# The scan of an RWKV-7 mixer: two recurrences side by side, another form of the recurrence, and other queues, banks and estimates

## The chip, the cores and the metric

The kernel runs on one core of one Trainium2 chip. The metric is the device time of one execution in microseconds (us), lower is better; the times shown are the median of several runs. TensorE (PE in the profile, PEld for its weight loads) multiplies matrices into PSUM, VectorE (DVE), ScalarE (ACT) and GpSimd (POOL) do the elementwise work, SyncE (SP) issues the DMA transfers.

## The reference

A four-layer encoder over 16 meta tokens and 512 tokens (T = 528 rows of 1024 features). The mixers of its layers are latent attention (MLA), RWKV-7, a gated linear recurrence and again MLA; behind each mixer comes a gated feed-forward network. The change is in the RWKV-7 mixer, whose heart is a recurrence over the tokens, for 16 heads of 64 features and in both directions:

```python
def _wkv7_scan(r, w, a, b, k, v, reverse):
    def step(S, inp):
        r_t, w_t, a_t, b_t, k_t, v_t = inp
        sa = jnp.einsum('bhvk,bhk->bhv', S, a_t)
        S = S * w_t[:, :, None, :] + sa[..., None] * b_t[:, :, None, :] + v_t[..., None] * k_t[:, :, None, :]
        return S, jnp.einsum('bhvk,bhk->bhv', S, r_t)
    ...
# in the mixer, for d in range(2):
        ys.append(_wkv7_scan(rf, decay, -kk, kk * a, kd, vf, reverse=(d == 1)))
        bonuses.append(jnp.sum(rf * kd * r_k_h, axis=-1, keepdims=True) * vf)
    y = ys[0] + ys[1]      # then normalised per head, plus the bonuses, gated, projected
```

## The kernel before

The kernel computes the recurrence in chunks of 64 tokens ("windows": NW = 8 full ones and a ninth of 16 tokens, N9 = 9). Two heads share the 128 partitions (a "pair", hp = 0 to 7; E[0] and E[1] are its halves), so a pair and a direction d make one **recurrence**, i = 2 hp + d, 16 in all. Nearly all its products are 64x64 by 64 columns in float32, one per head.

For each recurrence there are these streams of work, written as Python generators:

- `pair` loads r, k and v of two heads; `values` turns v to have tokens on partitions (vt).
- `stage_a` (line 1505) makes decays and the scaled r, a (xr) and b, k (bk), then in six PSUM banks the products of all tokens of a window with each other (am: for b and for k, against a and r), masked by VectorE.
- `a_tokens` turns a (at), `bk_tokens` turns b and k (tb), each with `turned`: a product with the identity per window and head, then copies on ScalarE. `ak_v` makes r1, am times v.
- `inverses` (line 1600) sends the 16x16 diagonal blocks of am through DRAM to 66 partitions (sc, bu), inverts them there in 30 small GpSimd operations (dt, dtmp) and sends them back (sd, dc).
- `stage_b` (line 1638) builds from dc the inverse X of the 64x64 triangle (dd, nn, xt) by four products in the one bank "rb", and xa = X times a.
- `chain` (line 1679) walks the nine windows. One step: u = X r1 + xa S (TensorE, then VectorE's copy), S' = decay times (S + k v + b u) (TensorE, then VectorE, with the product sp of S and the decay on GpSimd), and the output y from v, S and u in the bank "yp". `chain` of i waits for that of i - 1.
- `bonus` and `post` finish a pair.

**Order.** `Streams` (line 140 on) puts the streams into one program order per engine while the program is built: of the next operations of all streams it takes the one that by its estimates (`Op`: a cost by engine and size, LATENCY between engines, `after` for a DMA's landing) can start first, and among equals the one of highest priority (AHEAD[kind] - i). `take` and `give` hand out PSUM banks by kind; `wait` keeps a stream back until other streams are fully put in order. In line 1537 `stage_a` of i waits so for `chain` of i - DEEP; tiles of depth DEEP (xr, am, tb, pc) back it. On the chip each engine then runs its own list in order and waits where an operand is late. Where the estimates leave TensorE idle, `fill` puts in matmuls nobody reads, so far into a bank "idle" of their own. The eight PSUM banks are ps 3, ch 2, rb 1, yp 1, idle 1. The MLA mixers use the same `Streams` with their own streams. All DMA transfers are issued by SyncE, in the same program order.

Of the kernel before, what the change touches and what calls it, by code (L numbers as in the profile page):

```python
# [50 lines left out]
DEEP = 3  # L51
# [54 lines left out]
class Op:  # L106
    __slots__ = ("eng", "fn", "args", "kw", "outs", "ins", "cost", "work", "after", "mode")

    def __init__(self, eng, fn, name, args, kw):
# [6 lines left out]
        if eng == "pe":  # L116
# [27 lines left out]
class Streams:  # L144
# [19 lines left out]
    def wait(self, *names):  # L164
        return ("wait", names)
# [111 lines left out]
    def fill(self, start):  # L277
# [48 lines left out]
class Kern:  # L326
# [1034 lines left out]
    def rwkv_scan(self, es, hid, rkv, yall):  # L1361
# [14 lines left out]
        for kind, n in (("ps", 3), ("ch", 2), ("rb", 1), ("yp", 1)):  # L1376
# [4 lines left out]
        idle, dense = pp.tile([128, 512], F32, name="idle"), hid["w", 0]  # L1381
# [18 lines left out]
        xts = [cp.tile([128, N9, 64], F32, name=f"xt{j}") for j in range(2)]  # L1400
# [61 lines left out]
        def turned(src, out):  # L1462

            yield from per_window(lambda w, e: src(w)[E[e]], lambda w, e: self.ident[E[e], E[e]], lambda ps, ws: ac.copy(out[:, ws], ps))


        def pair(hp, P):
            if hp >= 2:
                yield wait(f"bonus{hp - 2}")
            for n, name in ((2, "v"), (0, "r")):  # L1470
                P[name] = tl([128, T], "in_" + name, 2)
                yield dq.dma_start(P[name], rkv[n, hp])
# [3 lines left out]
            yield dq.dma_start(P["k"], rkv[1, hp])  # L1476
# [28 lines left out]
        def stage_a(i, hp, d, P, U):  # L1505
            if i:
                yield wait(f"front{i - 1}")
            if d == 0:
                raw = tl([128, 512], "w2")
                yield dq.dma_start(raw, a["rw_2"][hp, :, 0:512])  # L1510
# [41 lines left out]
            yield spawn(f"at{i}", a_tokens(i, xr, U), prio("at", i))  # L1552
# [27 lines left out]
            yield spawn(f"r1{i}", ak_v(i, hp, P, U), prio("r1", i))  # L1580
            if d:
                yield po.tensor_tensor(out=P["kds"], in0=P["kds"], in1=kd, op=ALU.add)

        def a_tokens(i, xr, U):
            if i >= 2:
                yield wait(f"b{i - 2}")
            U["at"] = tl([128, N9, 64], "at", 2)
            yield from turned(lambda w: xr[:, 0, w * 64:w * 64 + 64], U["at"])
# [6 lines left out]
        def ak_v(i, hp, P, U):  # L1595
            yield wait(f"values{hp}", *([f"c{i - 3}"] if i >= 3 else []))
            r1 = U["r1"] = tl([128, N9, 64], "r1", 3)
# [336 lines left out]
```

## Time and profile before

| | us |
|---|---|
| median of 3 runs (3481.07 to 3485.17) | 3481.4 |
| the profiled execution | 3473.31 |
| its span, first to last instruction | 3471.5 |
| TensorE busy in the span | 3216.4 (93%) |
| VectorE busy | 2701.7 (78%) |
| ScalarE busy | 1673.0 (48%) |
| GpSimd busy | 936.7 (27%) |

The profile has one row per instruction: engine, line of the kernel, the tiles written and read (out<-in), start and length. The streams record their operations through one helper, so all of them have line L218, and tiles tell them apart. A float32 product shows as two TensorE instructions. TensorE's instructions overlap in its pipeline, so the distance between two starts is what one costs, not its length.

### The profile page before, as it was taken

The numbers are of one execution on the slowest core, as the hardware profiler recorded it, in microseconds if no ns is written. First come the engines' busy times: TensorE is split into PE (matmuls) and PEld (weight loads), VectorE is DVE, ScalarE is ACT, GpSimd is POOL, SyncE is SP. The second block draws the span as 40 slices with busy tenths as digits, with TensorE's granted clock in tenths as the row PEclk, the third lists the DMA queues.
The fourth block names the chain that finished last, engine by engine and source line by source line (L and its number), as shares of the span: only waits on it lengthen the run. The fifth ranks groups of instructions, "written<-read, shape, count | busy, mean of one in ns | idle before, by whom it ended". The sixth has DMA issues, their size and how long they took to land.

```text
span 3471.5 us, 77910 instructions
## 1 busy us (share of the span) xinstructions
PE 3216.4 (93%) x32057; PEld 3099.1 (89%) x32057; DVE 2701.7 (78%) x5006; ACT 1673.0 (48%) x3139; POOL 936.7 (27%) x1406
## 2 busy tenths in 40 slices
PE   7999999997988988879999988989999899989998
PEld 7899899996977878869999988989999799989998
DVE  6877789979336767657898788789886777788987
ACT  6665454433333333224544468654444666554443
POOL 0000143422016555433443200044331000034431
PEclk9999999998989999989999999999999999999999
DMA  2001223322322112113323222222322011112322
GB/s 84 34 33 40 84 71 104 99 87 88 136 69 50 35 40 45 25 42 102 98 95 107 80 73 74 80 73 88 106 86 83 21 38 35 65 64 83 101 93 72
DMA packets 157717, 250.07 MB, mean 72 GB/s; under 512 B 78736, under 2 KB 88112, under 8 KB 157232
## 3 DMA queue, kind: packets, MB, share of 16 engines
q1 hardware_dynamic: 157360, 245.08, 22.4%
q8 instruction: 252, 4.13, 0.5%
q14 instruction: 105, 0.86, 0.1%
HBM read 227.93 MB, written 17.10 MB: 71 GB/s over the span
## 4 chain that ended last, share of the span: by engine, by line
PE 47%; DVE 10%; ACT 6%; issue 2%; POOL 2%; DMA 2%; SPq 0%; DVEq 0%; ACTq 0%; POOLq 0%
PE bank L422 11%; PE bank L421 11%; PE bank L420 11%; PE pj L218 4%; PE ps L218 2%; PE s L218 1%; PE ch L218 1%; PE rb L218 1%; PE yp L218 1%; PE mm L420 1%; PE mm L421 1%; PE mm L422 1%; POOL dt L218 1%; ACT wv L218 1%; ACT th L1227 1%
## 5 line engine op out<-in xcount | busy, mean ns | idle before, releaser
L421 PE MATMUL bank<-xlo,whi 128*128 128x264 f32 x2272 | 655.7, 290 | 18.7 <-DVE xlo L562 10.9
L422 PE MATMUL bank<-xhi,wlo 128*128 128x264 f32 x2272 | 651.2, 289 | 12.4 <-DVE wlo L409 12.3
L420 PE MATMUL bank<-xhi,whi 128*128 128x264 f32 x2272 | 646.6, 289 | 15.4 <-ACT whi L408 13.8
L421 PEld LDWEIGHTS bank<-xlo,whi 128*128 128x128 f32 x2272 | 437.0, 192 | 26.1 <-DVE xlo L562 14.8
L420 PEld LDWEIGHTS bank<-xhi,whi 128*128 128x128 f32 x2272 | 432.7, 192 | 17.5 <-ACT whi L408 14.6
L422 PEld LDWEIGHTS bank<-xhi,wlo 128*128 128x128 f32 x2272 | 435.3, 192 | 14.4 <-DVE wlo L409 14.4
L422 PE MATMUL bank<-phi,wlo 128*128 128x264 f32 x1408 | 402.2, 286 | 0.0
L421 PE MATMUL bank<-plo,whi 128*128 128x264 f32 x1408 | 400.3, 284 | 0.0
L420 PE MATMUL bank<-phi,whi 128*128 128x264 f32 x1408 | 400.3, 284 | 0.0
L409 DVE TENSOR_TENSOR wlo<-wraw,whi 128x1024 fp32r<-128x1024 f32 (+1 forms) x234 | 262.8, 1125 | 116.0 <-ACT whi L408 115.8
L408 ACT CAST whi<-wraw 128x1024 fp32r<-128x1024 f32 (+1 forms) x234 | 222.4, 952 | 199.4 <-PE bank L421 157.8
L575 DVE TENSOR_TENSOR wlo<-wraw,whi 128x1024 fp32r<-128x1024 f32 (+1 forms) x216 | 286.3, 1326 | 29.7 <-ACT whi L574 28.1
L420 PEld LDWEIGHTS bank<-phi,whi 128*128 128x128 f32 x1408 | 265.4, 188 | 0.0
L422 PEld LDWEIGHTS bank<-phi,wlo 128*128 128x128 f32 x1408 | 264.9, 188 | 0.0
L421 PEld LDWEIGHTS bank<-plo,whi 128*128 128x128 f32 x1408 | 264.7, 188 | 0.0
L574 ACT CAST whi<-wraw 128x1024 fp32r<-128x1024 f32 (+1 forms) x216 | 195.2, 904 | 124.2 <-PE bank L421 72.4
L422 PE MATMUL bank<-thi,wlo 128*128 128x264 f32 x864 | 246.3, 285 | 0.0
L421 PE MATMUL bank<-tlo,whi 128*128 128x264 f32 x864 | 245.7, 284 | 0.0
L420 PE MATMUL bank<-thi,whi 128*128 128x264 f32 x864 | 244.9, 283 | 0.0
L589 POOL TENSOR_TENSOR wraw<-wraw,wsum 128x512 f32<-128x512 f32 x72 | 96.1, 1334 | 413.3 <-DVE wlo L575 368.2
L714 DVE SCALAR_TENSOR_TENSOR cv<-gp,par,cv 128x528 f32<-128x528 f32 x176 | 177.7, 1059 | 10.8 <-ACT cv L712 9.9
L422 PEld LDWEIGHTS bank<-thi,wlo 128*128 128x128 f32 x864 | 162.7, 188 | 0.4 <-DVE wlo L575 0.2
(403 smaller groups left out, 9708.2 us busy)
## 6 DMA issues: line engine op xcount, KB each, us to landing
wraw<-in_ffn_in_dram SPq DMA_DIRECT2D x176, 512.0 KB
wraw<-in_ffn_out_dram SPq DMA_DIRECT2D x96, 384.0 KB
wraw<-in_mla_o_dram SPq DMA_DIRECT2D x48, 256.0 KB
wraw<-in_rw_rkv_dram SPq DMA_DIRECT2D x24, 512.0 KB
wraw<-in_lru_in_dram SPq DMA_DIRECT2D x20, 512.0 KB
wraw<-in_mla_q_dram SPq DMA_DIRECT2D x16, 512.0 KB
wraw<-in_ffn_out_dram SPq DMA_DIRECT2D x16, 512.0 KB
rkv<-ro SPq DMA_DIRECT2D x24, 264.0 KB
```

What stands on the lines that cost most here:

```text
L218: op.fn(*op.args, **op.kw)
L408: nc.scalar.copy(hi[:, :cols], raw[:, :cols])
L409: nc.vector.tensor_tensor(out=lo[:, :cols], in0=raw[:, :cols], in1=hi[:, :cols].bitcast(F32), op=ALU.subtract)
L420: nc.tensor.matmul(out, lhsT=w[0][ws], rhs=x[0][xs], start=start, stop=False)
L421: nc.tensor.matmul(out, lhsT=w[0][ws], rhs=x[1][xs], start=False, stop=False)
L422: nc.tensor.matmul(out, lhsT=w[1][ws], rhs=x[0][xs], start=False, stop=stop)
L574: nc.scalar.copy(hi[:, cut], x[:, cut])
L575: nc.vector.tensor_tensor(out=lo[:, cut], in0=x[:, cut], in1=hi[:, cut].bitcast(F32), op=ALU.subtract)
L589: e.tensor_tensor(out=a1[:, 1], in0=a1[:, 1], in1=s[:, 1], op=ALU.subtract)
L714: nc.vector.scalar_tensor_tensor(out=c, in0=gp[:, q:q + T], scalar=self.p(f"fc_w{l}{q}", f), in1=c, op0=ALU.mult, op1=ALU.add)
L1227: nc.scalar.activation(out=self.two(v), in_=ps[:, :, :HT], func=AF.Tanh, scale=0.5, bias=z)
```

## The change

The recurrence takes another form: instead of r1 and xa made beforehand, a step makes W = am v + a S in PSUM, ScalarE copies it to x, and u = X x. `a_tokens`, `ak_v`, `turned` and the xa product go. b and k are turned by 128x128 transposes, five per operand, with copies of 64 partitions each. `chain` of i waits for that of i - 2, the last addition into y for that of i - 1, and the tiles of a recurrence (u, x, sp, s1) come twice. DEEP becomes 4, xt has three buffers. sp moves from GpSimd to ScalarE. PSUM: ps 3, ch 3, yp 2; `stage_b` takes its banks from ps, and fillers go into a ps bank that is free, if one is. The loads of v, r, k and of the second LoRA weights are issued on ScalarE's queue. Estimates: 64x64 products of few columns cost as much as of 64, GpSimd 290 ns and 1.95 ns an element, a DMA lands 2000 or 3000 ns later instead of 650.

```diff
-DEEP = 3
+DEEP = 4
@@ class Op
-                self.cost, self.work = 4 * max(n, m / 2) * (0.56 if self.mode == (64, 64) else 0.35 if m <= 32 else 1.0) / 2.3, 4 * n * rows
+                self.cost, self.work = 4 * max(n, m if self.mode == (64, 64) else m / 2) * (0.56 if self.mode == (64, 64) else 0.35 if m <= 32 else 1.0) / 2.3, 4 * n * rows
-                           "pool": (140, 2.1), "dma": (475, 0)}[eng]
-            self.cost = fixed + each * n
-        self.after = 650 + 4 * out.shape[0] * n / 360 if eng == "dma" else 0.0
+                           "pool": (290, 1.95), "dma": (475, 0)}[eng]
+            self.cost = 150 if name == "dma_start" and eng == "act" else fixed + each * n
+        self.after = (2000 if eng == "dma" else 3000) + 4 * out.shape[0] * n / 360 if name == "dma_start" else 0.0
@@ fill
-        while start - t > GAP and self.work < NEED:
+        while start - t > GAP and self.work < NEED and self.slots["ps"]:
-            self.warm(n)
+            self.warm(self.slots["ps"][0](), n)
@@ rwkv_scan
-        for kind, n in (("ps", 3), ("ch", 2), ("rb", 1), ("yp", 1)):
+        for kind, n in (("ps", 3), ("ch", 3), ("yp", 2)):
-        xts = [cp.tile([128, N9, 64], F32, name=f"xt{j}") for j in range(2)]
+        xts = [cp.tile([128, N9, 64], F32, name=f"xt{j}") for j in range(3)]
@@ pair (and the loads of w2 in stage_a and post alike)
-                yield dq.dma_start(P[name], rkv[n, hp])
+                yield ac.dma_start(P[name], rkv[n, hp])
@@ bk_tokens
-                yield from turned(lambda w: bk[:, j, w], tb[:, j])
...
+                ps = yield take("ps")
+                pv = ps.rearrange("p (w f) -> p w f", f=128)
+                for w in range(4):
+                    yield pe.transpose(pv[:, w], bk[:, j, 2 * w:2 * w + 2].rearrange("p w t -> p (w t)"), self.ident)
+                for w in range(2):
+                    for e in range(2):
+                        yield ac.copy(tb[E[e], j, w:NW:2], pv[E[w], :, E[e]])
+                yield give(ps)
+                ps = yield take("ps")
+                yield pe.transpose(ps[:64, 0:128], bk[:, j, NW], self.ident)
+                for e in range(2):
+                    yield ac.copy(tb[E[e], j, NW], ps[:64, E[e]])
+                yield give(ps)
@@ inverses
-            yield wait(*([f"c{i - 2}"] if i >= 2 else []))
+            yield wait(*([f"c{i - 3}"] if i >= 3 else []))
@@ stage_b (its xt part also waits for c{i - 3}, and xa goes)
-            yield wait(f"inv{i}", f"at{i}", f"r1{i}", *([f"b{i - 1}"] if i else []))
+            yield wait(f"inv{i}", *([f"b{i - 1}"] if i else []))
-                ps = yield take("rb")
+                ps = yield take("ps")
@@ chain
-            yield wait(f"b{i}", f"r1{i}", f"tb{i}", *([f"c{i - 1}"] if i else []))
+            yield wait(f"b{i}", f"values{hp}", f"tb{i}", *([f"c{i - 2}"] if i >= 2 else []))
-            yield from both(pu[:, 0:64], U["xt"][:, order[0]], U["r1"][:, order[0]], True, True)
+            yield from both(pw[:, 0:64], am[:, 1, order[0], 0:64], v[:, order[0]], True, True)
...
-                    yield from both(pu[:, 0:64], U["xa"][:, w], S, False, True)
+                    yield from both(pw[:, 0:64], xr[:, 0, w * 64:w * 64 + 64], S, False, True)
+                x = tl([128, 64], f"x{i % 2}", 2)
+                yield ac.copy(x, pw[:, 0:64])
+                yield give(pw)
...
-                        yield po.tensor_tensor(out=sp, in0=S, in1=p1.to_broadcast([128, 64]), op=ALU.mult)
+                        yield ac.activation(out=sp, in_=S, func=AF.Identity, scale=p1)
...
+                pu = yield take("ch")
+                yield from both(pu[:, 0:64], U["xt"][:, w], x, True, True)
                 yield ve.tensor_copy(u[:, w], pu[:, 0:64])
...
             if d:
+                yield wait(f"c{i - 1}")
                 yield ve.tensor_tensor(out=w64(y), in0=w64(y), in1=yp, op=ALU.add)
+                yield po.tensor_tensor(out=y[:, SEQ:], in0=y[:, SEQ:], in1=ye, op=ALU.add)
```

## Rows read from the trace of the kernel before

**Rows 1.** The page's first line.

```profile
span 3471.5 us, 77910 instructions
```

**Rows 2.** Stretches: window, its us, busy us (xinstructions) per engine, clock, DMA.

```profile
core 0: us, PE busy (x) PEld busy (x) DVE busy (x) ACT busy (x) POOL busy (x), PEclk, DMA share, GB/s
1060.00:1545.00 485.00, 426.16 (x9833) 387.43 (x9829) 320.62 (x862) 148.85 (x354) 247.38 (x627) 0.96 0.17 36
1200.00:1220.00 20.00, 18.01 (x504) 17.16 (x506) 10.99 (x40) 6.59 (x16) 10.96 (x34) 1.00 0.10 19
...
100.00:200.00 100.00, 96.50 (x762) 91.62 (x761) 80.86 (x180) 66.15 (x167) 4.00 (x3) 1.00 0.10 34
```

**Rows 3.** Tile u: all copies, then recurrences 6, 9, 15; "first to last start".

```profile
L218 DVE COPY u<-ch x144: 201/225/226, 1074.0 to 1541.7; 128x64 f32<-128x64 f32 x144
...
L218 DVE COPY u<-ch x9: 211/225/225, 1250.9 to 1278.7; 128x64 f32<-128x64 f32 x9
...
L218 DVE COPY u<-ch x9: 209/225/225, 1348.6 to 1371.4; 128x64 f32<-128x64 f32 x9
...
L218 DVE COPY u<-ch x9: 224/225/226, 1529.9 to 1541.7; 128x64 f32<-128x64 f32 x9
```

**Rows 4.** Timeline of recurrence 9 (start us, us): DVE, SP, ACT, in order.

```profile
1281.60 0.77 DVE L218 SCALAR_TENSOR_TENSOR xr<-kkh,ep 128x527 f32<-128x527 f32 x1
...
1294.12 1.24 SPq L218 DMA_DIRECT2D sc<-am  x2
...
1300.96 0.30 SPq L218 DMA_DIRECT2D bu<-sc  x1
...
1310.03 0.44 SPq L218 DMA_DIRECT2D in_k<-rkv  x1
...
1319.08 0.65 ACT L218 COPY dt<-dt 66x256 f32<-66x256 f32 x1 [4.04 <-POOL dt L218]
...
1322.14 0.37 SPq L218 DMA_DIRECT2D dc<-sd  x1
...
1346.38 0.70 ACT L218 COPY xa<-ps 128x512 f32<-128x512 f32 x2 [1.11 <-PE ps L218]
```

**Rows 5.** Waits in the scan: who <- whom: us in total, times, longest.

```profile
POOL sp L218 <- DVE s L218: 159.6, 67, 10.8
...
DVE kkh L218 <- DMA in_k<-rkv: 3.1, 4, 1.5
...
SPq L218 <- ACT dt L218: 165.2, 12, 21.0
```

**Rows 6.** Timeline of TensorE, short stretches of the scan and of an MLA mixer.

```profile
71.25 0.93 PE L218 MATMUL pj<-ident,p 128*128 128x128 f32 x7
...
1078.63 0.28 PE L218 MATMUL ch<-vt,tb 64*64 64x64 f32 x4
1078.85 0.72 PE L218 MATMUL ps<-rs_y,rwcst 128*128 128x132 f32 x4
1079.49 0.33 PE L218 MATMUL ch<-u,tb 64*64 64x64 f32 x4
...
1101.62 1.04 PE L218 MATMUL ps<-ident,bk 64*64 64x64 f32 x30
```

**Rows 7.** Groups by form, 993 to 1565 us: xcount | busy us, mean ns.

```profile
L218 POOL TENSOR_TENSOR sp<-s,pc 128x64 f32<-128x64 f32 x112 | 38.0, 340 | 161.5 <-DVE s L218 159.6 <-DVE xr L218 1.4 <-DVE h L218 0.3
...
L218 PE MATMUL ps<-xt,at 64*64 64x64 f32 x576 | 29.3, 243 | 6.2 <-DVE xt L218 4.8 <-ACT xa L218 0.7 <-DVE kkh L218 0.5
...
L218 ACT COPY vt<-ps 64x256 f32<-64x256 f32 x32 | 11.7, 366 | 6.1 <-PE ps L218 5.6
...
L218 ACT COPY xa<-ps 128x64 f32<-128x64 f32 x16 | 3.5, 221 | 1.5 <-PE ps L218 1.5
```

**Rows 8.** One step of a recurrence, timelines of VectorE and of TensorE.

```profile
1107.21 0.23 DVE L218 COPY u<-ch 128x64 f32<-128x64 f32 x1 [0.43 <-PE ch L218]
1107.97 0.28 DVE L218 SCALAR_TENSOR_TENSOR s<-ch,pc,sp 128x64 f32<-128x64 f32 x1 [0.54 <-PE ch L218]
...
1108.77 0.21 DVE L218 COPY u<-ch 128x64 f32<-128x64 f32 x1
...
1107.49 0.27 PE L218 MATMUL ch<-u,tb 64*64 64x64 f32 x1
```

More of the change, by code (lines that the diff above doesn't have):

```diff
@@ L1379, in rwkv_scan @@
         sch.slot("sq", lambda: tl([128, T], "sq"))
-        idle, dense = pp.tile([128, 512], F32, name="idle"), hid["w", 0]
+        dense = hid["w", 0]
         cst = cp.tile([128, a["rw_const"].shape[1]], F32, name="rwcst")
@@ L1592, in bk_tokens @@
             for j in range(2):
-                yield from turned(lambda w: bk[:, j, w], tb[:, j])
-        def ak_v(i, hp, P, U):
-            yield wait(f"values{hp}", *([f"c{i - 3}"] if i >= 3 else []))
-            r1 = U["r1"] = tl([128, N9, 64], "r1", 3)
-            yield from per_window(lambda w, e: U["am"][E[e], 1, w, 0:64], lambda w, e: P["vt"][E[e], w], lambda ps, ws: ac.copy(r1[:, ws], ps))
+                ps = yield take("ps")
[11 more added lines that the diff above has]
+                yield give(ps)
         def inverses(i, d, U):
@@ L1658, in stage_b @@
             yield give(ps)
-            if i >= 2:
-                yield wait(f"c{i - 2}")
-            xt = U["xt"] = xts[i % 2]
+            if i >= 3:
+                yield wait(f"c{i - 3}")
+            xt = U["xt"] = xts[i % 3]
             ps = yield from product(lambda w, e: nn[E[e], w], lambda w, e: dtr[E[e], w])
@@ L1673, in stage_b @@
                 yield give(ps)
-            xa = U["xa"] = tl([128, N9, 64], "xa", 2)
-            yield from per_window(lambda w, e: U["at"][E[e], w], lambda w, e: xt[E[e], w], lambda ps, ws: ac.copy(xa[:, ws], ps))
         def chain(i, hp, d, P, U):
-            yield wait(f"b{i}", f"r1{i}", f"tb{i}", *([f"c{i - 1}"] if i else []))
+            yield wait(f"b{i}", f"values{hp}", f"tb{i}", *([f"c{i - 2}"] if i >= 2 else []))
             am, xr, v, pc, y, tb = U["am"], U["xr"], P["vt"], U["pc"], yall[:, hp], U["tb"]
-            u = tl([128, N9, 64], "u")
+            u = tl([128, N9, 64], f"u{i % 2}")
             yt = yield take("yp")
@@ L1710, in chain @@
                     yield from both(ps[:, 0:64], tb[:, 0, w], u[:, w], False, True)
-                    pu = yield take("ch")
-                    yield from both(pu[:, 0:64], U["xt"][:, after], U["r1"][:, after], True, False)
-                    s1 = tl([128, 64], "s1", 3)
+                    pw = yield take("ch")
+                    yield from both(pw[:, 0:64], am[:, 1, after, 0:64], v[:, after], True, False)
+                    s1 = tl([128, 64], f"s1{i % 2}", 3)
                     if S is None:
@@ L1724, in chain @@
                 if w == NW:
-                    if d:
-                        yield ve.tensor_tensor(out=y[:, SEQ:], in0=y[:, SEQ:], in1=yo[:, 0:16], op=ALU.add)
-                    else:
-                        yield ac.copy(y[:, SEQ:], yo[:, 0:16])
+                    ye = tl([128, 16], "ye") if d else y[:, SEQ:]
+                    yield ac.copy(ye, yo[:, 0:16])
                     yield give(yo)
@@ L1785, in rwkv_scan @@
             sch.add(f"post{hp}", post(hp, P), prio("post", 2 * hp))
-        sch.warm = lambda n: nc.tensor.matmul(idle[:, 0:n], lhsT=dense[:, 0:128], rhs=dense[:, 0:n], start=True, stop=True)
+        sch.warm = lambda t, n: nc.tensor.matmul(t[:, 0:n], lhsT=dense[:, 0:128], rhs=dense[:, 0:n], start=True, stop=True)
         with tc.manual_schedule():
```

21 lines of the change are left out of this document (6 added, 15 removed).

## The prediction

> **What bounds the kernel now.** I read the span first: the profiled execution spans 3471.5 us [rows 1] and took 3473.3 us as a run, 8.1 us under the median of 3481.4 us. All sums below are made on 3473.3 and the 8.1 us are added back at the end.
>
> Next the stretches of time. The diff touches the scan, which lies between about 992 and 1562 us, and, through the scheduler's estimates alone, the two MLA mixers. In the steady part of the scan, 1060 to 1545 us, TensorE shows 426 of 485 us busy, but its matmuls are pipelined, so that is no measure of room. A better one is the count: 9833 instructions in 485 us, against 504 in the densest 20 us [rows 2]. At that densest pace they would need 9833 x 20/504 = 390 us. So some 95 us are not TensorE's own. VectorE is busy 320.6 us, ScalarE 148.9, GpSimd 247.4 [rows 2]. No engine is the bound by itself.
>
> Then who sets the pace. The copy into u marks each step of a recurrence: 144 of them, 9 per recurrence, 16 recurrences; first 1074.0, last 1541.7 [rows 3]. The last recurrence starts at 1529.9 us, so the 15 starts lie (1529.9 - 1074.0)/15 = 30.4 us apart. A start is late for this reason: stage_a of recurrence i waits in line 1537 until recurrence i - DEEP, here i - 3, has ended. I followed that loop for i = 9 [rows 3, 4]: recurrence 6 copies its last u at 1278.7; xr starts at 1281.6 (2.9 us later), am goes out to DRAM at 1294.1 (12.5), comes back at 1301.0 (6.8), GpSimd's block inverses end and dt is copied at 1319.1 (18.1), dc is fetched at 1322.1 (3.1), stage_b runs until xa is copied at 1346.4 (24.2), the first u follows at 1348.6 (2.2) and the last at 1371.4 (22.8). Sum 92.7 us, which is three starts of 30.9 us. The loop's length over its depth is the pace; the recurrence itself is 22.8 of the 92.7.
>
> **Recurrence depth and two at once.** The change makes the depth 4 and lets recurrence i start after i - 2. With 4 starts p to a loop, 4p = L + C. L, the way to the first u, is 69.9 us [rows 3, 4]. Two things leave it. The xa product and its copy: 36 instructions at 0.029 us (30 turns of bk take 1.04 us, less 0.22 for the last one, over 29 starts) [rows 6], two copies of 0.70 us together [rows 4], about 2 us with hand-overs. And GpSimd loses the sp products, which stand in order between the steps of the block inverses and wait for VectorE's s, 159.6 us in all [rows 5]; each takes 0.34 us [rows 7], so 7 take 2.4 us, and what the waits held up is between 0 and some 6 us. I take 3 for both. L = 65.
>
> C grows. A step is now 1.56 us where nothing disturbs it (u at 1107.21, next u at 1108.77) [rows 8]. The W form puts a product of X and a copy on ScalarE into each step: matmul to VectorE's start 0.48 us (1107.49 to 1107.97) [rows 8], the copy 0.22 us [rows 7], hand-over some 0.05: 0.75 us more, a factor of 1.48. So C = 22.8 x 1.48 = 34 us, if what else runs stretches the longer step as it does the present one. Two run side by side, so this asks only for 2p above 34, 17 us each, which does not bind. Then p = (65 + 34)/4 = 24.7 us.
>
> **TensorE's work.** Per recurrence it loses the xa product (576/16 = 36 instructions [rows 7]; the trace shows each float32 product as two, 9 windows of 2 heads), the turn of a, which has as many, and the 64x64 turns of b and k, twice as many (72); the product of am and v only moves into the recurrence. 144 x 0.029 = 4.2 us. It gains ten 128x128 transposes; seven in a row in an MLA mixer start 0.108 us apart (0.93 less the last one's 0.28, over 6) [rows 6], so 1.1 us. Between 64x64 work each group of them is a visit to another array mode. A visit of four matmuls shows its price: 0.22 us instead of 0.12 going in, 0.64 instead of 0.45 coming out [rows 6], 0.3 us. The Trainium skill, "TensorEngine Tiling (Array Packing)", section Tiling Modes, Key Properties, says that changing the tiling mode "drains the TensorE"; that speaks against turning b and k this way, and the row bears it out. Without any price of a visit the turns would gain 1.0 us a recurrence (72 x 0.029 - 1.1). With visits at 0.3 us, two (all joined) cost 0.6 and ten (each transpose alone) 3.0 us. I take three, 0.9 us, because the transposes of one bank stand together in the code. Net 4.2 - 1.1 - 0.9 = 2.2 us a recurrence, between 2.5 and 0.1.
>
> At the densest pace TensorE now needs 390/15.95 = 24.5 us a recurrence (485/30.4 = 15.95 recurrences), afterwards 22.3. So 24.7 us would be 90% of that pace, and VectorE, whose work hardly changes (320.6/15.95 = 20.1 us each), at 81%. Contention must lengthen the loop a little: I take p = 25.2 us, between 24.7 and 26.7.
>
> **ScalarE.** It is at 148.9/15.95 = 9.3 us a recurrence. The copies of at, xa and r1 go (3 x 0.8) and those of tb (2 x 0.8); twelve smaller ones come for tb (8 of about 0.37 [rows 7] and 4 of 0.2), 9 x copies of 0.22, 7 sp products between 0.22 and 0.34, and 40 load issues in all of 0.30 to 0.37 us as SyncE takes for one [rows 4], 0.9 us a recurrence. About 14 us of 25: no bound by load, but it now stands inside every step (a rival below).
>
> **Loads on ScalarE's queue.** SyncE's queue is in order and waits 165.2 us for the dt copy [rows 5]; the loads stand behind that, and so do sc and dc behind a load. But hardly anyone waits for a load: the first reader of k does so four times, 3.1 us in all [rows 5], since the pair is fetched a recurrence or more ahead; that is the work that hides them, and I price the move at 0. If that cover were gone, the 8 pairs would each wait some 3 us, the time dt to dc takes, 24 us. What moves with the loads are their waits for free buffers: they now hold up x copies instead of sc and dc, 0 to 1 us a pair.
>
> **Banks and fillers.** The bank of its own for stage_b and the idle bank go to ch and yp; stage_b's four products share the three ps banks. Price between 0 and 1 us a recurrence; I take 0, inside p. Fillers come only when a ps bank is free. The granted clock is 0.96 in the steady part [rows 2], so 4% of 485 us, 19 us, can be won by denser work, or as much lost if fillers fail. I take 0.
>
> **Estimates.** They change the order in both MLA mixers too. TensorE there is at 96.5 of 100 us at full clock [rows 2]; two mixers of some 350 us with 3.5% to win leave at most 25 us, and a worse order costs about as much. No row says which: 0, with 8 us either side.
>
> **Start and end.** The first recurrences are gated by nothing and come some 2 us closer together each; the last one, 11.8 us long now [rows 3], becomes 1.48 times as long, 5.7 us more. They cancel.
>
> **How the numbers follow.** Forecast: 15 x (30.4 - 25.2) = 78 us less, 3473.3 - 78 + 8.1 = 3403 us (24.7 to 26.7 with the other bounds: 3380 to 3435). Chance 0.50.
>
> Rivals:
> - **The engines set the pace, deeper.** TensorE and VectorE keep p at TensorE's dense pace, 22.3 us: 15 x 8.1 = 122 us less, 3360 us, down to 3345 with a clock that stays full. For: the loop at depth 4 falls if the block inverses go undisturbed. Against: 504 instructions in 20 us are the best of the scan, not its habit. Chance 0.15.
> - **Only the work comes off.** The loop's 70 us are themselves waits in TensorE's and VectorE's in-order queues and swell as soon as two recurrences run: stage_b takes 24.2 us for two multiplications, four products and xa [rows 4]. Then only 2.2 us a recurrence are left: 15 x 2.2 = 33, 3448 us. Chance 0.20.
> - **The price of ScalarE in the step.** Its order holds x copies behind waits, as for the dt copy after GpSimd or a load's free buffer (4.04 us ahead of the dt copy) [rows 4]. It decides when C passes 4 x 30.4 - 65 = 57 us, that is 7 us a step instead of the 4.2 that C = 34 means; one such 4 us wait in most steps would do it. At 8 us a step p is 32.3 and the time 3510 us, slower. For: the ends of GpSimd's work are hard to estimate. Against: such a wait comes once a recurrence, not once a step. Chance 0.07.
> - **No overlap.** The priorities run the older recurrence first and the younger one gets nothing; then a start costs C plus a hand-over, 34 + 3: 3580 us. Against: the older one waits at every hand-over. Chance 0.03.
> - **A wash** of fewer waits here and worse order there, within 0.2% (7 us, about what a measurement of this kernel tells from no change): 0.05.
>
> Faster by over 0.2%: 0.50 + 0.15 + 0.20 = 0.85; within 0.2%: 0.05; slower: 0.10. The range from 3345 to 3462 us leaves out the slower cases, the wash and the tails of the others, 0.2.
>
> **What would show it.** First u's about 25 us apart, with those of two recurrences mixed; xr of recurrence i just after the end of i - 4; no sp on GpSimd and less than 18 us between bu and the dt copy; steps of some 4 us; 134 fewer TensorE instructions a recurrence. It is wrong if xr starts well after recurrence i - 4 has ended (then the depth was not the gate), if starts stay 28 us or more apart, or if ScalarE shows long waits with x copies behind them.

## The result, and the profile after

The changed kernel takes **3503.9 us** (median of four runs, 3502.6 to 3510.7) beside 3481.2 us for the kernel before on the same chip: a ratio of 1.0063, interval 1.005 to 1.0075, some 22 us **slower**. The forecast was 3403, and its range ended at 3462. One execution of e10 (3945 us) and one of e16 (9108 us) were far slower than the others of their kernels and are left out of the ratios below.

The page after (engine lines: busy us, share, instructions); its execution took 3510.7 us, the slowest of the four, so the two traces differ by 37 us where the medians differ by 22.

```profile
span 3508.9 us, 73944 instructions
PE 3239.4 (92%) x29968; PEld 3088.0 (88%) x29968; DVE 2700.1 (77%) x4998; ACT 1727.8 (49%) x3435; POOL 904.8 (26%) x1303
```

TensorE has 2089 instructions fewer than before (x32057) and is busy 23 us longer. The stretches that answer to [rows 2]:

```profile
core 0: us, PE busy (x) PEld busy (x) DVE busy (x) ACT busy (x) POOL busy (x), PEclk, DMA share, GB/s
1060.00:1545.00 485.00, 424.64 (x7684) 365.65 (x7678) 310.78 (x824) 197.31 (x620) 221.00 (x532) 0.89 0.18 34
100.00:200.00 100.00, 96.32 (x767) 92.03 (x766) 81.44 (x181) 66.80 (x170) 3.98 (x3) 1.00 0.13 40
```

The MLA mixer is as before. In the scan TensorE is as busy as before (425 of 485 us) with 7684 instructions for 9833, at a granted clock of 0.89 for 0.96.

To place the loss I cut the scan at four rows: the load of its constants (993.7 us before, 993.6 after), the first state of the first and of the last recurrence (VectorE's scaling into s that takes no earlier state, once a recurrence), the last addition into y, and the first load of the saved h behind the scan. The second and third stand in one row, of before and then of after:

```profile
L218 DVE TENSOR_SCALAR s<-ch,pc x16: 269/276/286, 1076.6 to 1530.6; 128x64 f32<-128x64 f32 x16
```

```profile
L218 DVE TENSOR_SCALAR s<-ch,pc x16: 272/280/285, 1089.6 to 1546.8; 128x64 f32<-128x64 f32 x16
```

In us, with kernels explained below (rest: from that load to the end of the span):

| kernel | to the first state | 15 starts | last recurrence | to the next load | rest |
|---|---|---|---|---|---|
| before | 82.9 | 453.9 | 11.9 | 12.6 | 1916.5 |
| after | 96.0 | 457.2 | 24.8 | 14.7 | 1922.6 |
| e1, fillers of a gap in one tile | 95.0 | 436.2 | 21.6 | 12.7 | 1915.9 |
| e5, e1 with the old estimates | 80.9 | 433.1 | 19.9 | 13.2 | 1918.9 |

So the loop, from which 78 us were to come off, is 3 us longer; 13 us come at the start, 13 in the last recurrence, 2 behind it and 6 in the rest, where an execution 7 us above its median stands beside one 8 us below. Recurrence 9, to be read against [rows 4] (a "..." for what lies between):

```profile
1283.95 0.68 DVE L218 TENSOR_TENSOR h<-h,yp 128x512 f32<-128x512 f32 x1
...
1285.95 0.80 DVE L218 SCALAR_TENSOR_TENSOR xr<-kkh,ep 128x527 f32<-128x527 f32 x1
...
1300.39 0.58 SPq L218 DMA_DIRECT2D sc<-am  x1
...
1308.05 0.30 SPq L218 DMA_DIRECT2D bu<-sc  x1
...
1331.76 0.61 ACT L218 COPY dt<-dt 66x256 f32<-66x256 f32 x1
...
1337.28 0.38 SPq L218 DMA_DIRECT2D dc<-sd  x1
...
1374.27 0.28 DVE L218 TENSOR_SCALAR s<-ch,pc 128x64 f32<-128x64 f32 x1
...
1411.52 0.69 DVE L218 TENSOR_TENSOR h<-h,yp 128x512 f32<-128x512 f32 x1 [0.28 <-PE yp L218]
```

The addition into y that ends recurrence 5 starts at 1283.95, and xr of 9 starts 2.0 us later: the gate is the one foreseen. But the way from there to the first state is 88.3 us. The same pieces as means over recurrences 4 to 13 (all from start to start; gate: from the addition into y of i - DEEP to xr; L: xr to first state; C: first state to the addition into y):

| kernel | gate | xr to sc | sc to bu | bu to dt copy | dt to dc | dc to state | L | C | sum / depth |
|---|---|---|---|---|---|---|---|---|---|
| before | 4.6 | 12.3 | 6.7 | 18.4 | 3.1 | 29.9 | 70.3 | 23.2 | 32.7 |
| after | 1.4 | 15.7 | 8.5 | 28.2 | 3.6 | 35.7 | 91.6 | 35.1 | 32.0 |
| e1 | 1.4 | 15.1 | 8.2 | 27.6 | 3.5 | 35.0 | 89.4 | 34.1 | 31.2 |
| e5 | 2.6 | 17.1 | 5.4 | 19.7 | 3.1 | 33.3 | 78.6 | 39.7 | 30.2 |
| e7, e1 at depth 3 | 1.4 | 14.4 | 7.3 | 31.0 | 3.8 | 25.7 | 82.3 | 27.7 | 37.1 |
| e9, e5 with half the fold | 8.3 | 13.2 | 7.3 | 11.5 | 3.2 | 32.4 | 67.6 | 46.9 | 30.7 |
| e17, e5 with more products | 4.5 | 13.9 | 6.4 | 17.9 | 3.4 | 32.1 | 73.7 | 46.9 | 31.3 |

### The profile page after: what moved, and what is told of

Same layout as the page of the kernel before. It is cut to its first block, busy times and chain, and to the rows that moved or that the text cites. A ratio compares the mean times of both kernels' runs of the same rounds, so it can differ in the third digit from the quotient of the medians.

```text
span 3508.9 us, 73944 instructions
## 1 busy us (share of the span) xinstructions
PE 3239.4 (92%) x29968; PEld 3088.0 (88%) x29968; DVE 2700.1 (77%) x4998; ACT 1727.8 (49%) x3435; POOL 904.8 (26%) x1303
## 4 chain that ended last, share of the span: by engine, by line
PE 72%; DVE 15%; ACT 10%; issue 3%; DMA 0%; POOL 0%; ACTq 0%; SPq 0%; DVEq 0%; POOLq 0%
PE bank L422 16%; PE bank L420 16%; PE bank L421 16%; PE pj L218 8%; PE ps L218 5%; PE s L218 2%; PE ch L218 2%; PE ps L1782 1%; ACT tb L218 1%; ACT wv L218 1%; DVE pst L218 1%; PE yp L218 1%; ACT p L218 1%; PE mm L421 1%; PE mm L422 1%
## 5 line engine op out<-in xcount | busy, mean ns | idle before, releaser
L421 PE MATMUL bank<-xlo,whi 128*128 128x264 f32 x2272 | 653.9, 289 | 19.3 <-DVE xlo L562 11.5
L422 PE MATMUL bank<-xhi,wlo 128*128 128x264 f32 x2272 | 649.3, 288 | 13.9 <-DVE wlo L409 13.9
L409 DVE TENSOR_TENSOR wlo<-wraw,whi 128x1024 fp32r<-128x1024 f32 (+1 forms) x234 | 263.1, 1125 | 121.5 <-ACT whi L408 121.0
L575 DVE TENSOR_TENSOR wlo<-wraw,whi 128x1024 fp32r<-128x1024 f32 (+1 forms) x216 | 286.4, 1326 | 29.9 <-ACT whi L574 28.1
```

Source lines behind the costliest of these rows:

```text
L409: nc.vector.tensor_tensor(out=lo[:, :cols], in0=raw[:, :cols], in1=hi[:, :cols].bitcast(F32), op=ALU.subtract)
L421: nc.tensor.matmul(out, lhsT=w[0][ws], rhs=x[1][xs], start=False, stop=False)
L422: nc.tensor.matmul(out, lhsT=w[1][ws], rhs=x[0][xs], start=False, stop=stop)
L575: nc.vector.tensor_tensor(out=lo[:, cut], in0=x[:, cut], in1=hi[:, cut].bitcast(F32), op=ALU.subtract)
```

## Experiments

Each ratio is to the kernel before, run on the same chip; 0.001 is 3.5 us, and differences between kernels are taken from the ratios.

### Fillers

In the changed kernel every filler takes a new tile of a ps bank. All rows of line 1782 (duration least, median, longest; first to last start), and from the waits of 1060 to 1560 us (total, times, longest) the one that goes with them:

```profile
L1782 PE MATMUL ps<-hid_w x96: 279/580/583, 992.6 to 1579.7; 128*128 128x256 f32 x96
```

```profile
PEld ps L1782 <- PE ps L1782: 10.8, 35, 0.4
```

There are 96 of them (41 before), and 35 times in this stretch the weight load of a filler waits until the filler ahead of it has ended. **e1** gives the fillers of one gap one tile, with the order of all else unchanged:

```diff
-        while start - t > GAP and self.work < NEED and self.slots["ps"]:
+        into = self.slots["ps"][0]() if start - t > GAP and self.work < NEED and self.slots["ps"] else None
+        while into is not None and start - t > GAP and self.work < NEED:
...
-            self.warm(self.slots["ps"][0](), n)
+            self.warm(into, n)
```

> The changed kernel with one difference: all fillers of one gap go into one tile of a ps bank, instead of a new tile for each filler. Every engine's order stays the same. Theory F (the fillers cost the time): in the changed kernel a filler starts 0.44 to 0.64 us after the one before it, because each opens its own tile and waits until the last one has ended; 96 of them, 50.6 us from filler to next start, where 41 took 15.6 us before. With one tile per gap they come 0.12 us apart again; 66 of the 96 follow another one, so 66 x 0.35 = 23 us of TensorE time come free and the granted clock rises: 3504 - 23 to 3504 - 40, so 3465 to 3480 us. Theory Q (ScalarE's order lengthens the loop; fillers only fill time that nobody needs): 3498 to 3510 us.

Measured 3478.3 us, ratio 0.9987 (0.9978 to 0.9996): 26 us less than the changed kernel. One and the same gap, of after and then of e1:

```profile
1069.17 1.86 PE L1782 MATMUL ps<-hid_w 128*128 128x256 f32 x3 [1.48 <-ACT tb L218]
```

```profile
1068.10 1.01 PE L1783 MATMUL ps<-hid_w 128*128 128x256 f32 x3 [1.38 <-ACT tb L218]
```

Over all 96 the distances from a filler to the next instruction (each counted to 0.7 at most) sum to 49.5 us in after, 0.44 to 0.64 for most, and to 24.1 in e1, 0.11 to 0.22 for most.

**e2** does the reverse to the kernel before:

```diff
-        while start - t > GAP and self.work < NEED:
+        while start - t > GAP and self.work < NEED and self.slots["ps"]:
-            self.warm(n)
+            self.warm(self.slots["ps"][0](), n)
```

> The kernel before with one difference: its fillers go into ps banks, a new tile for each, as in the changed kernel. Order unchanged, 41 fillers. Theory F: 33 of them follow another filler and now wait for it, 33 x 0.35 = 12 us more, 3490 to 3498 us. Theory Q: within 4 us of the kernel before, because 17 of the 41 lie in the scan's start, where TensorE waits for data anyway, and so do the last 9.

Measured 3492.0, ratio 1.0021 (1.0011 to 1.003): 7 us more with 41 fillers, whose distances grow from 8.8 to 20.5 us.

**e13**, **e14** and **e15** take all fillers out of the changed kernel, of e5 and of the kernel before:

```diff
-NEED = 4300
+NEED = 0
```

> The changed kernel without any filler (the planned order of all other instructions stays as it is). Its 96 fillers take 49.5 us of TensorE's queue in the trace, 3503.9 with them. Theory F2 (TensorE runs behind its plan, so the fillers stand in no gap at all and each pushes all that follows): the time falls by their full length, to about 3454, which is also 24 below the 3478 of the kernel with one tile a gap. Theory K (they keep the granted clock up, 0.90 to 0.94 in the loop, and so pay for a part of themselves): without them the granted clock falls to 0.85 or less, TensorE's 430 us in the loop get 5 to 10% longer, and the time is 3470 to 3500.

> The kernel of e5 (W form, old estimates, one tile a gap: 3463.5) without any filler. Its 48 fillers take 11.7 us in the trace. Theory F2: 3463.5 - 12 = 3452, and close to the changed kernel without fillers, since the estimates act mostly through the number of fillers. Theory K: 3465 to 3480, at a lower granted clock. If the estimates act through the order itself, this kernel stays 15 below the changed kernel without fillers.

> The kernel before without any filler. Its 41 fillers take 8.8 us in the trace, 3482.5 with them. Theory F2: 3473. Theory K: 3483 to 3495, at a lower granted clock. Set beside the changed kernel without fillers, it gives what the rest of the change is worth.

Measured 3481.7 (ratio 1.0008, 0.9996 to 1.0019), 3463.6 (0.9953, 0.9936 to 0.997) and 3483.2 (1.001, 0.9996 to 1.0023). Against e1, e5 and the kernel before that is 7, 4 and 3 us more. So F2 falls: fillers that aren't serialised cost nothing net. That they gain something isn't shown, since the intervals of e5 and e14 overlap, that of e15 takes in 1, and those of e1 and e13 touch. The granted clock from 1180 to 1480 us goes from 0.94, 0.93 and 0.95 with fillers to 0.91, 0.92 and 0.95 without, a smaller fall than theory K said.

### Estimates

**e4** puts only the new estimates into the kernel before:

```diff
-... 4 * max(n, m / 2) * ...
+... 4 * max(n, m if self.mode == (64, 64) else m / 2) * ...
-"pool": (140, 2.1)
+"pool": (290, 1.95)
-        self.after = 650 + 4 * out.shape[0] * n / 360 if eng == "dma" else 0.0
+        self.after = 2000 + 4 * out.shape[0] * n / 360 if eng == "dma" else 0.0
```

> The kernel before with the new estimates alone (64x64 products of few columns, GpSimd's fixed and per-element time, 2000 instead of 650 ns for a DMA's landing), in the scan and in both MLA mixers. Theory E (the estimates themselves cost time, since operations that wait for a DMA are put later in every queue): slower by 10 us or more. Theories F and Q: the estimates are not the cause; the order gets a little better or worse, 3470 to 3490 us.

Measured 3525.1, ratio 1.0119 (1.0104 to 1.0134): 41 us more, nearly all in the loop:

```profile
L218 DVE TENSOR_SCALAR s<-ch,pc x16: 257/283/286, 1081.8 to 1581.4; 128x64 f32<-128x64 f32 x16
```

499.6 us for 15 starts, where before had 453.9.

**e5** is e1 with the three old estimates:

```diff
-... m if self.mode == (64, 64) else m / 2 ...
+... m / 2 ...
-"pool": (290, 1.95)
+"pool": (140, 2.1)
-        self.after = (2000 if eng == "dma" else 3000) + ...
+        self.after = 650 + ...
```

> The changed kernel with all fillers of one gap in one ps tile (3478.3 in an earlier run) and, besides, the scheduler's three old estimates (GpSimd 140 + 2.1, a DMA's landing 650, small products of a 64x64 visit by half their columns). Theory E: the new estimates set the order of the scan's instructions badly, whatever the form; on the kernel before they cost 41 us (3525.1 against 3484.4). If the same order defects come with the W form, this kernel is near 3478 - 41 = 3437, and the loop's first u copies lie about 28 apart where they lay 29.3 apart. Rival E0: the estimates were fitted to the W form (its own plan, with four recurrences deep), and putting the old ones back leaves the time at 3478 within 5, or makes it slower by up to 20.

Measured **3463.5**, ratio 0.9942 (0.9925 to 0.9958): 16 us under e1, less than the 41 of theory E, and the fastest kernel that leaves nothing out, with e14 beside it: 20 us under the kernel before, 42 under the changed one. The gain isn't where e4 lost: the way to the first state is 14 us shorter, the loop only 3. Without fillers on either side (e14 against e13) the old estimates are worth 19 us, so it is the order that they give and not the number of fillers.

**e11** and **e12** are e1 with one of the three put back, GpSimd's and the DMA's:

```diff
-"pool": (290, 1.95)
+"pool": (140, 2.1)
```

```diff
-        self.after = (2000 if eng == "dma" else 3000) + ...
+        self.after = 650 + ...
```

> The changed kernel with all fillers of one gap in one ps tile (3478.3), and of the three estimates only GpSimd's put back (140 + 2.1 per element instead of 290 + 1.95). With all three put back the time was 3463.5. In the traces the old estimates shorten GpSimd's fold and the wait of its last copy (22.4 to 16.7 us) above all. Theory G: the dearer GpSimd is what sets the fold's instructions late and behind others, so this one alone gives most of the 15 us: 3463 to 3468. Rival: the DMA estimate does it, and this one alone leaves 3478 within 4.

> The changed kernel with all fillers of one gap in one ps tile (3478.3), and of the three estimates only the DMA's put back (a landing 650 ns after the issue, instead of 2000 on SyncE's queue and 3000 on ScalarE's). With all three put back the time was 3463.5. Theory D: with the longer landing the scheduler believes the fold and stage b to start later than they can, and sets ScalarE's and VectorE's other work ahead of them; this one alone gives most of the 15 us: 3463 to 3468. Rival: GpSimd's estimate does it, and this one alone leaves 3478 within 4.

Measured 3468.1 (0.9957, 0.9942 to 0.9972) and 3488.3 (1.0016, 1.0006 to 1.0026): GpSimd's alone gives 10 of the 16 us, the DMA's alone makes it 10 us slower. They don't add up; each is another order.

### Parts of the change, one at a time

**e3**, the changed kernel with the two dt copies on GpSimd (`ac.copy` becomes `po.tensor_copy`), since ScalarE's copy starts 6 us after the fold's end (mean of recurrences 3 to 14, 0.1 before):

```diff
-            yield ac.copy(x.rearrange("p s t -> p (s t)"), id16)
+            yield po.tensor_copy(x.rearrange("p s t -> p (s t)"), id16)
...
-            yield ac.copy(dt[:, 1], dt[:, 0].rearrange("p s t -> p t s"))
+            yield po.tensor_copy(dt[:, 1], dt[:, 0].rearrange("p s t -> p t s"))
```

> The changed kernel with one difference: the two copies of the block inverses' tile dt (its start value, and its transposed form at the end) are GpSimd's instead of ScalarE's. In the changed kernel the last copy starts 6.0 us after GpSimd has ended dt (mean of recurrences 3 to 14; 0.1 us before the change), since on ScalarE's queue it stands behind x copies that wait for TensorE; and GpSimd starts dt 7.6 us after the load of bu is issued (3.0 before). Theory Q: the way from xr to the first u falls by some 10 of 95 us, the loop over four recurrences by as much, 2.5 us a start, 15 x 2.5 = 37 us: 3460 to 3480 us. Theory F: within 6 us of 3504.

Measured 3512.0, ratio 1.008 (1.0064 to 1.0097), 6 us more than the changed kernel. A wait of 6 us a recurrence was taken away and no time was gained. In its trace bu to the dt copy is 3.3 us shorter and the copy to dc 3.9 us longer (24.9 and 7.5, means as in the table).

**e6**, e1 with one recurrence at a time:

```diff
-            yield wait(f"b{i}", f"values{hp}", f"tb{i}", *([f"c{i - 2}"] if i >= 2 else []))
+            yield wait(f"b{i}", f"values{hp}", f"tb{i}", *([f"c{i - 1}"] if i else []))
```

> As the changed kernel with all fillers of one gap in one ps tile (3478.3), but the chain of a recurrence waits for the chain right before it instead of the one before that, so that no two recurrences run at once; the x, sp, u, s1 tiles and the banks stay as they are. Theory O (the traces showed first u copies 29 apart and chains of 32 to 35 that overlap by about 5 us each): without the overlap the starts lie a whole chain apart; a chain alone would take about 30, its ScalarE copy being on it, so 15 x (30 to 33 - 29.3) = 10 to 55 us more: 3490 to 3530, most likely about 3505. Rival: the overlap carries nothing since stage a's way to the chain ends last for each recurrence: 3478 within 6.

Measured 3521.0, ratio 1.0106 (1.0091 to 1.0121): the overlap is worth 41 us.

**e7**, e1 with `DEEP = 3`:

```diff
-DEEP = 4
+DEEP = 3
```

> As the changed kernel with all fillers of one gap in one ps tile (3478.3), but the buffers of am, xr, dtr and tb let stage a run 3 recurrences ahead instead of 4. Theory L (the loop is 4p = L + C with L the way from the gate to the first u, and L swells when stages of more recurrences lie beside each other): with 3 the loop is 3p = L + C; if L stays at 95, p = (95 + 33)/3 = 42.7 and the time is 15 x 13 = 200 us more, 3680; if L falls back to the 65 to 70 of the kernel before, p = 33, 15 x 4 = 60 us more, 3538. Rival: L is only the spare time of a queue whose real limit is a busy engine or the chain itself; then the gate was never what ended last and the time stays at 3478 within 10.

Measured 3571.0, ratio 1.025 (1.0235 to 1.0265): the depth is worth 92 us, between the two ends of theory L; L falls by only 7 us (table). The scheduler planned both kernels anew, with 159 (e6) and 210 fillers (e7) for e1's 96, so neither price is that of the one line alone.

**e8**, e1 with the loads back on SyncE's queue (`ac.dma_start` becomes `dq.dma_start` in `pair`, `stage_a` and `post`):

```diff
-                yield ac.dma_start(P[name], rkv[n, hp])
+                yield dq.dma_start(P[name], rkv[n, hp])
```

> As the changed kernel with all fillers of one gap in one ps tile (3478.3), but the loads of v, r, k and the W2 halves go back to SyncE's queue. Theory N (the queue that issues the loads ends no wait that the scan's end hangs on): 3478 within 6. Rival: a load that stands behind SyncE's scatter waits of the fold (165 us of waits on that queue before) comes late and stage a with it: 3488 to 3510. Other rival: ScalarE is relieved of 33 issues and its dt copies come sooner: 3460 to 3470.

Measured 3484.8, ratio 1.0 (0.999 to 1.001): 4 us more than e1, with intervals that overlap by little.

**e16**, e5 with b and k turned by 64x64 products again:

```diff
-                    yield pe.transpose(pv[:, w], bk[:, j, 2 * w:2 * w + 2].rearrange("p w t -> p (w t)"), self.ident)
...
+                yield from turned(lambda w: bk[:, j, w], tb[:, j])
```

> The kernel of e5 (3463.5) with b and k turned by 64x64 products as in the kernel before, instead of by 128x128 transposes. The turns by 128x128 take 10 transposes at 0.108 and 12 ScalarE copies at 367 and 202 ns in a recurrence, with some 3 changes of TensorE's mode each way; the small ones take 36 products, 72 instructions at 29 ns = 2.1 us, and 6 copies (four of 128x256 and two of 128x64). Theory M (ScalarE's copies and the mode changes of the large turns cost as much as the products they save): 3463 within 5. Theory T (the products that they save are TensorE's own time on the path): the small turns are 16 x (2.1 - 1.1) = 16 slower, 3480. Rival: x copies stand behind the twelve small copies on ScalarE, and with six copies instead the chain is shorter: 3445 to 3455.

Measured 3476.5, ratio 0.9986 (0.9969 to 1.0004): 15 us more than e5, near theory T. Its trace is of its fastest run, 10 us under the median, and only 4 us longer than e5's, with 15 starts as long (432.4 us); so where the 15 us go isn't shown.

**e18**, e5 with the scaled state back on GpSimd:

```diff
-                        yield ac.activation(out=sp, in_=S, func=AF.Identity, scale=p1)
+                        yield po.tensor_tensor(out=sp, in0=S, in1=p1.to_broadcast([128, 64]), op=ALU.mult)
```

> The kernel of e5 (3463.5) with the scaled state sp back on GpSimd (340 ns each there, 352 ns on ScalarE), 112 of them in all. Theory S (ScalarE's sp stands in front of the next x copies and of the dt copies, which are on the way from the gate to the first u): without it the time falls by 5 to 15 us, 3449 to 3458. Rival (GpSimd's sp stands between the fold's steps, 159.6 us of waits of sp behind s in the kernel before, and lengthens the fold): 3466 to 3480. Third: neither ends last, 3463 within 3.

Measured 3468.3, ratio 0.9954 (0.9935 to 0.9973): 4 us more than e5, with intervals that overlap. Theory S falls; the run doesn't tell the rival (3466 to 3480) from the third case.

### What paces the loop

**e9**, e5 with half of GpSimd's fold left out:

```diff
-            for j in range(15):
+            for j in range(0, 15, 2):
```

> The kernel of e5 (W form, fillers of a gap in one tile, old estimates: 3463.5), but GpSimd's fold of the 16x16 blocks leaves out 7 of its 15 steps (every second one stays), so the inverses are wrong by what these steps add. It takes 7 of the 15 us of GpSimd's stretch (about 1 us a step in e5's trace) out of the way from the gate to the first u, and nothing from TensorE, VectorE or ScalarE. Theory L (the loop is 4p = L + C and each us of L ends last): L falls from 79 to 72 and the time by 15 x 7/4 + 7 = 33 us, to 3430. Theory P (TensorE's queue, busy 88% of this stretch, sets the pace, and L and C only stretch to fill it): the time falls by the 7 us of the first recurrence at most: 3456 to 3463.

Measured 3461.0, ratio 0.9938 (0.9921 to 0.9954), 1 us under e5, as theory P said. The way from bu to the dt copy is 8.2 us shorter and L 11, but the gate is 5.7 us longer and C 7.2 (table). Its trace is of its fastest run, 9 us under the median; the first state comes 10 us sooner there than in e5's. The 15 starts, of e5 and then of e9:

```profile
L218 DVE TENSOR_SCALAR s<-ch,pc x16: 270/276/285, 1075.3 to 1508.4; 128x64 f32<-128x64 f32 x16
```

```profile
L218 DVE TENSOR_SCALAR s<-ch,pc x16: 271/276/284, 1064.9 to 1499.5; 128x64 f32<-128x64 f32 x16
```

They take 433.1 and 434.6 us.

**e10**, e5 without two of the three output products:

```diff
-                yield from both(yo[:, 0:n], v[:, w], am[:, 1, w, 64:64 + n], True, False)
-                if S is not None:
-                    yield from both(yo[:, 0:n], S, rw, False, False)
-                yield from both(yo[:, 0:n], u[:, w], am[:, 0, w, 64:64 + n], False, True)
+                yield from both(yo[:, 0:n], u[:, w], am[:, 0, w, 64:64 + n], True, True)
```

> The kernel of e5 (3463.5), but the chain leaves out two of the three products that make the output of each window (v with the masked block, and the state with r), so the output lacks these terms. They are 68 instructions of a 64x64 tile per recurrence, 29 ns apart, 2.0 us of TensorE's queue, 31 us in all sixteen, and nobody in the loop waits for them. Theory P (TensorE's queue sets the pace): the time falls by about 31 us, to 3432. Theory L (the loop of gate, L and C sets it): 3463 within 8, since they are on neither L nor C except where they stand in front of something.

Measured 3476.0, ratio 0.9976 (0.9966 to 0.9986): 12 us **more** than e5 with 31 us of products less. The stretch of [rows 2], of e5 and then of e10:

```profile
1060.00:1545.00 485.00, 410.77 (x7979) 358.68 (x7973) 316.64 (x866) 206.77 (x650) 212.43 (x519) 0.92 0.18 37
```

```profile
1060.00:1545.00 485.00, 415.13 (x6999) 354.29 (x6997) 313.95 (x853) 202.48 (x645) 217.19 (x528) 0.88 0.18 34
```

TensorE is as busy with 980 instructions fewer: 59.3 ns each (415.13/6999) against 51.5. Some 3 of these 8 ns come from the mix alone, since the instructions left out are short ones: by 29 ns each, an estimate gives (410.77 - 1054 x 0.029)/(7979 - 1054) = 55 ns without them. The mean granted clock of 0.88 is 24% of the stretch at the lower of the two levels, 1.2 of 2.4 GHz ((1 - 0.88)/0.5), against 16%: 39 us more at half speed, by which some 19 us of work are lost (an estimate) of the some 30 taken out. The scheduler also put in 122 fillers for 48, 31.6 us for 11.7 by their distances; in this stretch 99 for 25, 27.4 us for 7.5. So e10 isn't a pure test: no run leaves out these products and the fillers too.

**e17** adds products instead:

```diff
+                for _ in range(2):
+                    yield from both(yo[:, 0:n], v[:, w], am[:, 1, w, 64:64 + n], True, True)
                 yield from both(yo[:, 0:n], v[:, w], am[:, 1, w, 64:64 + n], True, False)
```

> The kernel of e5 (3463.5) with the first product of each window's output (v with the masked block) computed three times into the same place, so the output is the same: 72 more instructions of a 64x64 tile per recurrence, 29 ns apart, 2.1 us, 33 us in all sixteen. Nobody in the loop waits for them. Theory P (TensorE's queue, with its breaks between groups of four, sets the pace): 33 us more, 3497, or some less where the granted clock rises with them (0.93 in e5's loop): 3485 to 3500. Theory L (latency sets the loop): within 8 of 3463. With e10 (the mirror: 31 us of products less, 12 us slower at 0.85) a rise here says that TensorE's time counts and the clock hid the saving there; no rise says that TensorE's queue has the room.

Measured 3479.5, ratio 0.999 (0.9977 to 1.0004): 17 us more, half of the 33 us added.

```profile
1060.00:1545.00 485.00, 421.83 (x9104) 375.93 (x9098) 312.99 (x848) 201.26 (x640) 211.44 (x518) 0.95 0.18 35
```

At 0.95 an instruction takes 46.3 ns. Neither theory holds alone: latency taken out gives nothing, of TensorE's work added half counts, and e10 lies outside both forecasts.

## Why the prediction was wrong, point by point

The 22 us, by the ratios: serialised fillers +26 (after against e1), new estimates +16 (e1 against e5), all else -20 (e5 against before). The forecast had 0, 0 and -78, so the loop is the largest part of the miss, 58 of 100 us, and the first two turned the sign.

- **Fillers: a step that failed, 26 us.** "Fillers come only when a ps bank is free", priced at 0, counted the bank and not the tile. The diff shows that each filler makes a tile of its own, and with two tiles of one bank the second waited for the first (the wait shown above). The 19 us "either way" were a size for the clock, not for that. e1 and e2 show it.
- **Estimates: 0, 8 either way, a step that failed, 16 us.** I looked for their effect in the MLA mixers, which lie as before, and not in the scan, the stage with the most waits between engines. There they cost 16 to 19 us, and 41 on the form before (e4, e5, e13, e14). No view of the trace gives such a price; the bound should have been as wide as the loop's waits.
- **The gate: right.** In the changed kernel xr starts 1.4 us after the addition that ends i - 4, and one depth less costs 92 us. In e9 and e16 the gate is 8.3 and 8.5 us, so there something besides the depth holds xr back.
- **C = 34: right for the changed kernel** (35.1, steps of 35.1/8 = 4.4 us where some 4 were foreseen). But there two recurrences overlap by only some 5 us (starts are 30.5 apart); in e5, with more overlap, C is 39.7.
- **L = 65: wrong, the step that failed for the loop.** It is 91.6, and 78.6 with fillers and estimates put right. Neither reduction came. Without xa, dc to the first state is 33.3 us (e5) for 29.9; without sp on GpSimd, bu to the dt copy is 19.7 for 18.4. In e5 the gate (2.6), L (13.6 more) and C (5.7 more) make 21.9 us, 5.5 a start. Part of it was lost in the reading: by the prediction's own marks (last u of i - DEEP to first u of i) L is 74.9 us before as a mean of these recurrences, not the 69.9 of recurrence 9; by the same marks it is 92.8 after and 80.6 in e5. Over the whole loop a start takes 433.1/15 = 28.9 us where I took 25.2, 55 of the missing 58 us. Two signs that the prediction named for its being wrong came: starts 28 us or more apart (30.5 after), and bu to the dt copy not under 18 us (28.2).
- **TensorE's capacity: taken too large; that this is the reason under L is argued, not shown.** The instruction count was right to one: 2089 on the page and 55 more fillers, 134 a recurrence. But I took the densest 20 us, 39.7 ns an instruction [rows 2], for what TensorE can do throughout, and so left room. The busy time per instruction was 43.3 ns before and is 55.3 after, 51.5 in e5; the prediction's own prices give 49 from the changed mix (an estimate: (426.2 - 15.95 x 3.1)/(9833 - 15.95 x 134)). Counted over 1180 to 1480 us, distances of 70 to 260 ns from one instruction to the next fill 102 us before (807 of them) and 126 in e5 (968); 88 of these, 12.4 us, follow the new 128x128 transposes, so half of the growth is work and not waiting. I called denser work a gain for the clock; fewer instructions in the same waits went with a lower one (0.96 before, 0.92 in e5).
- **Turns of b and k: better than forecast.** Forecast 0.1 us gained per recurrence (72 x 0.029 - 1.1 - 0.9), up to 1.0 without visits; e16 gives 15 us in all, about 1, so no price of the visits shows in it. The rule of the Trainium skill ("TensorEngine Tiling (Array Packing)", Tiling Modes, Key Properties) that a change of mode drains TensorE did not decide against them.
- **ScalarE: right that it is no bound by load.** Of after, 1060 to 1560 us (who waits for whom: total, times, longest):

```profile
ACT x L218 <- PE ch L218: 182.2, 87, 6.2
...
PEld ch L218 <- ACT x L218: 16.1, 39, 1.0
...
PE ch L218 <- ACT x L218: 10.1, 32, 0.9
```

  ScalarE waits for TensorE, hardly the other way round. Of ScalarE's own work the path does hold some (the table below). The scaled state takes 352 ns there, just above my 0.22 to 0.34. The Trainium skill ("ScalarE: Activation LUTs", What ACT_TABLE_LOAD costs) gives 186 ns plus 0.833 an element and 93 for a pointer operand, an estimate of 332 for these 64, which the trace bears out within 20 ns. Moved back to GpSimd it gains nothing (e18).
- **Loads: 0, measured 4 us gained**, at the edge of the intervals.
- **Start and end: did not cancel.** The last recurrence is 8 (e5) to 13 us longer for 5.7, and in the changed kernel the first state comes 13 us later, which the old estimates undo.
- **The rivals.** The 0.10 for slower lay on ScalarE's step and on no overlap; neither happened. Of the mechanisms named, "only the work comes off" (3448) is nearest to what the form does once fillers and estimates are right (3463.5), and its reason, waits in in-order queues that swell with two recurrences, is what e9's table shows. It had 0.20.

**Open** is what holds 15 starts at 432 to 436 us in e1, e5, e8, e9, e11, e14 and e16 (e10, e12, e13, e17 and e18 have 441 to 451). TensorE's queue with its pauses and its clock is the best supported reading (e9, half of e17, the clock in e10), but e16 has 483 more TensorE instructions than e5 from 1180 to 1480 us and the same loop, which it doesn't explain. The profile's chain of the work that ended last, cut to these 300 us, tells what the path was made of (share of the stretch in %):

| kernel | TensorE | VectorE | ScalarE | GpSimd and DMA |
|---|---|---|---|---|
| before | 37 | 29 | 2 | 26 |
| after | 55 | 22 | 17 | 1 |
| e1 | 51 | 24 | 19 | 1 |
| e5 | 38 | 20 | 13 | 21 |
| e16 | 33 | 18 | 3 | 40 |

In the changed kernel the fold and its transfers are hardly on the path any more; TensorE's order and ScalarE's copies (of tb above all, 8%) are, so that microseconds taken from the fold could not come back one for one. In e16 the path is the fold's again, at the same pace, so no single engine is shown to hold it. Untested is the price of the banks, 0 in the prediction: no run gives stage_b its own bank back. Nor is it shown by which instructions an estimate makes an order bad.

## What to carry to other kernels

A change that touches a scheduler's estimates or its filler instructions is a change to every stage it orders: price it in the stage with the most hand-overs, and read from the code which tile a filler writes, since a new tile of the same bank each time is a chain. A loop that runs through in-order queues has no fixed latency (e7, e9): before crediting a microsecond taken from it, ask which queue would then be waiting, and do not take the densest stretch of an engine for its capacity. Undo such side changes one by one; here two of them hid a form that is 20 us faster.

## What the runs showed of the hardware

- Taking products off TensorE went with a lower granted clock (0.92 to 0.88) and more fillers, so that its busy time rose from 410.8 to 415.1 us with 980 instructions fewer (e5, e10); adding products went with 0.95, and 421.8 us for 1125 instructions more (e17).
- A 128x256 product into a new tile of the same bank mostly starts 0.44 to 0.64 us after its predecessor (after), into the same tile 0.11 to 0.22 (e1).
- Filler products that follow each other freely cost nothing net: leaving them out made three kernels 3 to 7 us slower, mostly within the intervals (e13 to e15).
